# Latent attention: how the reciprocal softmax sums of two items reach the partitions of the output, by transposes or by way of DRAM

## The chip, the cores and the metric

One core of one Trainium2 chip runs the whole kernel. The metric is the device time of one execution in microseconds (us). Before the change it is 2557.08 us, the median of 3 runs (2555.43 to 2558.92).

## The reference, cut to what matters

The layer is a half-step SwiGLU, two token mixers side by side (2-D neighbourhood attention and latent attention, MLA), their gated merge, and another half-step SwiGLU, in float32. The change lies in the latent attention alone:

```python
def _attend(q, k, v):
    s = jnp.einsum('bqhd,bkhd->bhqk', q * q.shape[-1] ** -0.5, k).astype(jnp.float32)
    p = jax.nn.softmax(s, axis=-1).astype(v.dtype)
    return jnp.einsum('bhqk,bkhd->bqhd', p, v)
...
    o_mla = _blocked_attention(q_mla, k_mla, v_mla)
```

There are 8 heads, 1024 latent queries, 1280 keys (256 of context and 1024 latent), 96 channels in a query and a key, and 64 in a value.

## The kernel before, in words

Both attentions run in one loop over 64 **items** (`todo`): items 0 to 31 are neighbourhood attention (8 heads of 4), items 32 to 63 are latent attention (8 heads of 4 blocks of 256 queries). An item has three stages, and the loop overlaps them. In pass n of the loop, the values stage of item n is issued in five parts; between the parts the scores stage of item n+3 (`AHEAD = 3`) is issued, also in five steps; and the softmax steps of item n+2, which its scores stage left in the list `soft` one pass earlier, are handed out over the parts. So a latent item m has its scores in pass m-3, its exponentials in pass m-2 and its values in pass m.

*Scores* (`MlaItem.scores`): the first step multiplies the 256 queries with the context keys, into one bank of PSUM, and needs the tiles of `qh`, `ql` and `kvc`. The next four steps multiply with the latent keys, two halves for each 128 queries, and need `kh` and `kl` too. Each product is three matmuls, since every operand is held as a high and a low part. VectorE copies each bank to SBUF and takes row maxima on the way (`copy_max`, line 1966).

*Softmax*: four exponentials on ScalarE (line 2105) sum their rows as they go; `total` adds the sums and takes the reciprocal on VectorE (lines 2108 and 2109). Two items, 2k and 2k+1, share one 128 x 4 tile of reciprocals, `sums`: queries on partitions, and four columns for two items of two times 128 queries. The sum is not applied to the probabilities but to the output, at the end.

*Values* (`MlaItem.values`): each part transposes four 128 x 128 blocks of probabilities on TensorE (line 164), ScalarE copies them to SBUF as the high part (line 2131), VectorE makes the low part (line 2132), and two parts later (`LAG = 2`) TensorE multiplies them with the values (line 161, tile `bv`). After the fifth part, `head_out` finishes the item: the output stands with value channels on 64 partitions and queries along the row, so the reciprocals, which stand with queries on partitions, have to be turned into a row of 256 and repeated on 64 partitions.

Before, this goes in three steps for a pair of items. GpSimd widens the 128 x 4 tile to 128 x 256 (`widen`, line 1954; it is put in an unused tile named `rope`). In `head_out` of the even item, TensorE transposes it in two pieces into the free half of the output's PSUM bank (lines 1931 and 1932), and two copies bring the two items' rows to SBUF (lines 1934 and 1935). Then, for both items, a copy and an addition join the output's two halves (lines 1938 and 1939), and GpSimd multiplies with the row and splits the result (lines 1940 to 1943). Copies are on ScalarE, in the last four items on VectorE.

*Loads.* All DMAs are issued by SyncE (SP), one after the other in the order in which they are written down; a DMA that has to wait holds back those behind it. `MlaHead` issues fourteen of them for a head: twelve for queries and keys (`qh`, `ql`, `kvc`, `kh`, `kl`), the last two of which are `kl`, and two for values. It is called in pass n where n is a multiple of 4, for the next head, whose first scores are in pass n+1. The query and key tiles (pool `w`, and `kc` or `x`) have room for two heads, so SyncE can issue a head's loads as soon as the head before the last has done its last scores, a whole head ahead of their use. Tile names in the profile are those of the pools: `w`, `kc`, `x`, `l`, `p`, `z` are tiles of a head, `bs`, `bm`, `bv` banks of PSUM, `xu` and `t` working tiles, `st` small columns, `d` scratch in DRAM.

A scheduler places the instructions of each engine from this program; TensorE's and SyncE's keep the written order in this stage, while VectorE's and ScalarE's may be moved a few places.

Of the kernel before, what the change touches and what calls it, by code (L numbers as in the profile page):

```python
# [8 lines left out]
F32 = mybir.dt.float32  # L9
# [6 lines left out]
P = 128  # L16
# [6 lines left out]
NH = 8  # L23
# [15 lines left out]
def f32(ap):  # L39
    return ap.bitcast(F32)  # L40
# [3 lines left out]
def hybrid_block(ctx: ExitStack, tc: tile.TileContext, a: dict, out: bass.AP):  # L44
# [9 lines left out]
    pools = {}  # L54

    def nm(s):
        count[0] += 1
        return f"{s}_{count[0]}"

    def open_pool(key, name, bufs, side):  # L60
        pools[key] = tc.alloc_tile_pool(name=nm(name), bufs=bufs, side=side, reuse_waits="tile")

    def close_pools(*keys):
        for key in keys:
            pools.pop(key).release()

    def U(dt=F32, key="u"):
        return pools[key].tile([P, 1024], dt, tag="u", name=nm("x" + key))
# [7 lines left out]
    def T2(dt=F32, n=512):  # L76
        return pools["t"].tile([P, n], dt, tag="t", name=nm("t"))

    def ST(n=1):
        return sp.tile([P, n], F32, tag=f"st{n}", name=nm("st"))  # L80

    def DR(shape):
        n = nm("d")
        return dp.tile(shape, F32, tag=n, name=n)
# [3 lines left out]
    def PB(tag):  # L88
        return ps.tile([P, 512], F32, tag=tag, name=nm("b" + tag), bufs=PBUFS[tag])
# [17 lines left out]
    def pin(i):  # L107
        if pinned[0]:
            tc.keep_in_program_order(i)
        return i  # L110
# [20 lines left out]
    def put(dst, src):  # L131
        return pin(nc.sync.dma_start(dst, src))
# [30 lines left out]
    def turn_(o, x, i):  # L163
        return pin(nc.tensor.transpose(o, x, i))  # L164

    def mm3(o, s, m, start, stop):
        mmul(o, s[0], m[0], start=start, stop=False)
        mmul(o, s[0], m[1], start=False, stop=False)
        mmul(o, s[1], m[0], start=False, stop=stop)
# [1076 lines left out]
    o = len(plan.main)  # L1246
# [64 lines left out]
    o = len(plan.main)  # L1311
# [12 lines left out]
    o, tail = down1.plan(plan)  # L1324
# [111 lines left out]
    def emit_lat(d, ci, x, bank):  # L1436
        t, sq = T2() if bank else x, T2()

        def high():
            if bank:  # L1440
                act.copy(t, x)
            store(cqT[d][:, ci * 512:(ci + 1) * 512], t)
            act.activation(sq, t, AF.Square)
            later(add, 1)

        def add():
            if ci in squares:
                vec.tensor_tensor(squares[ci], squares[ci], sq, op=ALU.add)
            else:
                squares[ci] = sq  # L1450
        later(high)

    for p in range(3):
        punits.append(Unit(h2, [wc_cols(2 * p), wc_cols(2 * p + 1)],
                           lambda i, ci, x, bank, p=p: emit_lat(2 * p + i, ci, x, bank)))
# [21 lines left out]
    o = len(plan.main)  # L1477
# [137 lines left out]
    o = len(plan.main)  # L1615
# [139 lines left out]
    def na_loads(h):  # L1755
        heads["na", h] = x = NaHead()
        yield from x.loads(h)
# [97 lines left out]
    o = va_at  # L1855
# [9 lines left out]
    o = len(plan.main)  # L1865
# [4 lines left out]
    o = len(plan.main)  # L1870
# [3 lines left out]
    o = len(plan.main)  # L1874
# [3 lines left out]
    o = len(plan.main)  # L1878
# [6 lines left out]
    def na_next(h, n=1):  # L1885
        if h not in na_open:
            na_open[h] = na_loads(h)
        for _ in range(n):
            next(na_open[h], None)
# [31 lines left out]
    def head_out(pv, n, h, hi, lo, shape):  # L1921

        b, c = (0, 64) if h % 2 == 0 else (64, 0)
        copy = nc.vector.tensor_copy if n >= len(todo) - 4 else nc.scalar.copy
        t = T2()
        o, rb = t[b:b + 64, :256], t[b:b + 64, 256:512]
        if n % 2 == 0:  # L1930
            for i in range(2):
                turn_(pv[:, 256 + i * P:256 + (i + 1) * P], wide(n)[:, i * P:(i + 1) * P], ident)
            other = held[0] = T2()
            copy(rb, pv[0:64, 256:512])
            copy(other[b:b + 64, :256], pv[64:128, 256:512])
        else:
            rb = held[0][b:b + 64, :256]
        copy(o, pv[c:c + 64, :256])  # L1938
        nc.vector.tensor_tensor(o, o, pv[b:b + 64, :256], op=ALU.add)
        nc.gpsimd.tensor_tensor(o, o, rb, op=ALU.mult)  # L1940
        o = shape(o)
        nc.gpsimd.tensor_copy(hi[b:b + 64], o)
        nc.gpsimd.tensor_tensor(lo[b:b + 64], o, f32(hi[b:b + 64]), op=ALU.subtract)

    sums, held = {}, [None]

    def wide(n):

        return rope.rearrange("p a b -> p (a b)")[:, (n // 2) % 2 * 256:(n // 2) % 2 * 256 + 256]

    def widen(n):

        x = sums[n // 2].rearrange("p (x i o) -> p i x o", i=2, o=1).to_broadcast([P, 2, 2, 64])
        nc.gpsimd.tensor_copy(wide(n).rearrange("p (i x c) -> p i x c", i=2, x=2), x)

    def sums_of(n):
        if n // 2 not in sums:
            sums[n // 2] = ST(4)
        return sums[n // 2][:, (n % 2) * 2:(n % 2) * 2 + 2]
# [5 lines left out]
    def copy_max(dst, src, m):  # L1965
        nc.vector.tensor_scalar(dst, src, 1.0, FMIN, op0=ALU.mult, op1=ALU.max, accum_out=m)  # L1966
# [5 lines left out]
    class NaItem:  # L1972
# [3 lines left out]
        def scores(self):  # L1976
# [30 lines left out]
            if self.n % 2:  # L2007
                soft.append(lambda: widen(self.n))
            yield

        def values(self):
# [36 lines left out]
            def edge():  # L2048
                turned(((0, 0), (1, 2)), eh, el)

                def w():
                    weigh(pv[0], vt(0), [x[:, 0:256] for x in (eh, el)], False, False)
                    weigh(pv[0], vt(3), [x[:, 128:384] for x in (eh, el)], False, True)
                    hi, lo = [o.rearrange("p (s r j c) -> p s r j c", s=2, r=8, j=4)[:, :, :, j, :] for o in ona[h // 2]]
                    head_out(pv[0], self.n, h, hi, lo, lambda t: t.rearrange("p (s r c) -> p s r c", s=2, r=8))
                return w
# [22 lines left out]
    class MlaItem:  # L2079
# [3 lines left out]
        def scores(self):  # L2083
            hd, b = self.head, self.b
            cx = PB("s")
            m, n_, l, r = ST(8), ST(2), ST(4), sums_of(self.n)
            self.prl, self.prc = prl, prc = [U(), U()], T2()
            qq = [[x[:QK, b * 256 + s * P:b * 256 + (s + 1) * P] for x in (hd.qh, hd.ql)] for s in range(2)]
            for s in range(2):
                mm3(cx[:, s * 256:(s + 1) * 256], qq[s], [hd.kvc[:QK, 0:256], hd.kvc[:QK, 256:512]], True, True)  # L2090
            for s in range(2):
                copy_max(prc[:, s * 256:(s + 1) * 256], cx[:, s * 256:(s + 1) * 256], m[:, 3 * s + 2:3 * s + 3])
            yield
            for s in range(2):
                for e in range(2):
                    lat = PB("s")
                    mm3(lat, qq[s], [x[:QK, e * 512:(e + 1) * 512] for x in (hd.kh, hd.kl)], True, True)
                    copy_max(prl[s][:, e * 512:(e + 1) * 512], lat, m[:, 3 * s + e:3 * s + e + 1])
                    if s + e < 2:
                        yield  # L2100
            nc.vector.tensor_reduce(n_, m[:, 0:6].rearrange("p (s c) -> p s c", s=2), axis=AX.X, op=ALU.max, negate=True)

            def exp(x, i):
                s = i % 2
                nc.scalar.activation(x, x, AF.Exp, bias=n_[:, s:s + 1], accum_out=l[:, i:i + 1])  # L2105

            def total():
                nc.vector.tensor_tensor(r, l[:, 0:2], l[:, 2:4], op=ALU.add)
                nc.vector.reciprocal(r, r)

            for s in range(2):
                soft.append(lambda s=s: exp(prl[s], s))
                soft.append(lambda s=s: exp(prc[:, s * 256:(s + 1) * 256], 2 + s))
            soft.append(total)
            if self.n % 2:
                soft.append(lambda: widen(self.n))
            yield

        def values(self):
# [28 lines left out]
    soft, started = [], []  # L2148
# [25 lines left out]
    close_pools("u", "t")  # L2174
    open_pool("o", "heads", 16, "right")
    open_pool("p", "values", 2, "right")
    na_next(0)
    open_pool("t", "half", 12, "right")
    open_pool("u", "units", 10, "right")
# [81 lines left out]
        fm.step()  # L2261
    pinned[0] = False

    close_pools("u", "t", "p", "z", "x", "y", "l", "kc", "w")
    open_pool("t", "half", TBUFS, "left")
    open_pool("u", "units", 24, "left")

# [41 lines left out]
    for d in range(KD):  # L2309
        o = len(plan.main)  # L2310
# [52 lines left out]
    o = len(plan.main)  # L2363
# [13 lines left out]
    o = len(plan.main)  # L2377
# [14 lines left out]
    o, tail = down2.plan(plan)  # L2392
# [134 lines left out]
```

## Time and profile before

| what | value |
| --- | --- |
| median of 3 runs | 2557.08 us (2555.43 to 2558.92) |
| profiled execution, first to last instruction (its span) | 2553.0 us; it has no other time of its own |
| granted TensorE clock, mean | 0.999 |
| TensorE matmul, busy | 2524.7 us (99%) |
| TensorE weight load, busy | 2146.5 us (84%) |
| VectorE, busy | 1904.4 us (75%) |
| ScalarE, busy | 1238.4 us (49%) |
| GpSimd, busy | 239.4 us (9%) |
| chain of waits, share of TensorE | 87% |

Times in the profile are counted from the start of the span. The latent items fill about 1454 to 1740 us of it. "PE" is a matmul of TensorE, "PEld" its weight load, DVE VectorE, ACT ScalarE, POOL GpSimd, SPq SyncE's queue of DMAs. The median of the runs lies 4.1 us above the profiled execution's span.

### The profile page before, as it was taken

How to read it: one execution, taken by the hardware profiler on the slowest of the kernel's cores; microseconds unless marked ns; L12 is line 12 of the kernel's file. 1: busy time of each engine (PE TensorE's matmuls, PEld its weight loads, DVE VectorE, ACT ScalarE, POOL GpSimd, SP SyncE). 2: the span in 40 equal slices, each digit the busy share in tenths (PEclk: the TensorE clock that was granted, in tenths of full speed). 3: DMA queues.
4: the chain of work that ended last, by engine and by line, in shares of the span. 5: the costliest groups of instructions: out<-in, count | busy, mean ns of one | idle time of the engine just before them, and what ended most of it. 6: DMA issues, size and time to landing. Idle time of an engine off the chain costs nothing.

```text
span 2553.0 us, 38188 instructions
## 1 busy us (share of the span) xinstructions
PE 2524.7 (99%) x13007; PEld 2146.5 (84%) x13007; DVE 1904.4 (75%) x3652; ACT 1238.4 (49%) x2384; POOL 239.4 (9%) x421
## 2 busy tenths in 40 slices
PE   8999999999999999999999999999999999999998
PEld 6888888888888888889889999988888888888887
DVE  5788887898567687874568988886445888777557
ACT  6622223555346643433438888772355322233633
POOL 1000000000002200001006622220030000000000
PEclk9999999999999999999999999999999999999999
DMA  8477765779576665666899823205135667557655
GB/s 314 161 244 234 243 224 188 274 247 294 182 241 221 245 224 188 226 229 203 277 284 249 233 67 77 77 28 214 67 131 179 212 223 236 183 185 259 240 202 194
DMA packets 275477, 523.33 MB, mean 205 GB/s; under 512 B 33425, under 2 KB 84433, under 8 KB 275281
## 3 DMA queue, kind: packets, MB, share of 16 engines
q1 hardware_dynamic: 275280, 520.88, 61.3%
q8 instruction: 103, 1.69, 0.3%
q14 instruction: 94, 0.76, 0.1%
HBM read 375.47 MB, written 145.29 MB: 204 GB/s over the span
## 4 chain that ended last, share of the span: by engine, by line
PE 87%; ACT 5%; DVE 4%; issue 2%; DMA 1%; SPq 0%; POOL 0%; DVEq 0%; POOLq 0%; ACTq 0%
PE bs L161 33%; PE bm L161 30%; PE bv L161 20%; PE bm L164 2%; ACT xu L2105 2%; PE bs L164 1%; DVE xu L1966 1%; DVE t L2132 1%; ACT t L2131 1%; ACT xu L2004 1%; DVE xv L120 1%; DMA xv<-in_wada 0%; ACT t L2105 0%; ACT t L1938 0%; PE bv L164 0%
## 5 line engine op out<-in xcount | busy, mean ns | idle before, releaser
L120 ACT CAST xu<-t 128x512 fp32r<-128x512 f32 x589 | 345.6, 618 | 669.8 <-DVE t L120 556.1
L161 PE MATMUL bm<-xu,xu 128*128 128x512 f32 (+1 forms) x2442 | 596.5, 389 | 0.5 <-ACT t L120 0.4
L161 PEld LDWEIGHTS bm<-xu,xu 128*128 128x128 f32 x2442 | 450.4, 188 | 91.6 <-ACT t L120 1.7
L120 DVE TENSOR_TENSOR xu<-t,xu 128x512 fp32r<-128x512 f32 x589 | 382.8, 686 | 78.3 <-ACT xu L120 78.0
L161 PE MATMUL bs<-xu,xu 128*128 128x512 f32 (+2 forms) x1581 | 388.4, 385 | 0.0
L161 PE MATMUL bs<-xv,xu 128*128 128x512 f32 x1512 | 363.6, 390 | 0.2 <-DVE t L120 0.2
L161 PEld LDWEIGHTS bs<-xu,xu 128*128 128x128 f32 x1581 | 291.9, 188 | 57.8
L161 PE MATMUL bv<-xv,xu 128*128 128x512 f32 x1342 | 336.1, 390 | 0.0
L161 PEld LDWEIGHTS bs<-xv,xu 128*128 128x128 f32 x1512 | 283.6, 188 | 59.5 <-issue 1.0
L161 PEld LDWEIGHTS bv<-xv,xu 128*128 128x128 f32 x1342 | 251.7, 188 | 51.9
L120 DVE TENSOR_TENSOR xu<-xu,xu 128x512 fp32r<-128x512 f32 x282 | 189.5, 687 | 59.9 <-ACT xu L120 58.9
L120 DVE TENSOR_TENSOR t<-t,t 128x512 f32<-128x512 f32 (+4 forms) x350 | 221.0, 634 | 13.9 <-ACT t L120 8.7
L161 PE MATMUL bv<-xu,xu 128*128 128x512 f32 x722 | 191.5, 390 | 0.0
L120 ACT CAST xu<-xu 128x512 fp32r<-128x512 f32 x282 | 169.2, 619 | 15.2 <-DMA xu<-in_f1w 8.9
L120 POOL TENSOR_SCALAR st<-st 128x1 f32<-128x1 f32 x56 | 23.8, 425 | 1581.9 <-ACT t L120 1234.4
L161 PEld LDWEIGHTS bv<-xu,xu 128*128 128x128 f32 x722 | 135.6, 188 | 28.0
L161 PE MATMUL bm<-t,xu 128*128 128x256 f32 (+1 forms) x920 | 156.9, 333 | 0.0
L161 PEld LDWEIGHTS bm<-t,xu 128*128 128x128 f32 x920 | 137.7, 189 | 18.3
L161 PE MATMUL bs<-w,w 96*128 96x512 f32 (+1 forms) x384 | 145.0, 406 | 3.9 <-DVE st L1995 2.1
L2132 DVE TENSOR_TENSOR t<-bm,t 128x512 fp32r<-128x512 f32 x160 | 109.6, 687 | 28.5 <-ACT t L2131 28.1
L164 PE MATMUL bm<-ident,xu 128*128 128x128 f32 x826 | 126.5, 272 | 0.0
L1966 DVE TENSOR_SCALAR_CACHE_REDUCE xu<-bs 128x512 f32<-128x512 f32 (+1 forms) x186 | 110.2, 599 | 2.3 <-PE bs L161 2.1
(256 smaller groups left out, 3376.3 us busy)
## 6 DMA issues: line engine op xcount, KB each, us to landing
d<-t SPq DMA_DIRECT2D x432, 256.0 KB, 2.9
t<-d SPq DMA_DIRECT2D x348, 256.0 KB, 4.9
xu<-in_f1w SPq DMA_DIRECT2D x104, 512.0 KB, 4.4
xu<-in_f2w SPq DMA_DIRECT2D x58, 512.0 KB, 4.6
t<-in_wada SPq DMA_DIRECT2D x112, 256.0 KB, 4.9
t<-in_f1w SPq DMA_DIRECT2D x77, 256.0 KB, 4.8
t<-in_f2w SPq DMA_DIRECT2D x77, 256.0 KB, 5.2
xu<-in_winT SPq DMA_DIRECT2D x36, 512.0 KB, 5.4
```

The source lines that it names most:

```text
L120: return lambda *x, **y: pin(f(*x, **y))
L161: return pin(nc.tensor.matmul(o, s, m, start=start, stop=stop, skip_group_check=open_group[0]))
L164: return pin(nc.tensor.transpose(o, x, i))
L1966: nc.vector.tensor_scalar(dst, src, 1.0, FMIN, op0=ALU.mult, op1=ALU.max, accum_out=m)
L2004: soft.append(lambda s=s: nc.scalar.activation(pr[s][:, :640], pr[s][:, :640], AF.Exp, bias=n_[:, s:s + 1], accum_out=l[:, s:s + 1]))
L2105: nc.scalar.activation(x, x, AF.Exp, bias=n_[:, s:s + 1], accum_out=l[:, i:i + 1])
L2131: nc.scalar.copy(t[0], pb)
L2132: nc.vector.tensor_tensor(t[1], pb, f32(t[0]), op=ALU.subtract)
```

## The change

For the latent items, `widen` and the two transposes with their two copies go. In their place, when the odd item's reciprocals are there, `spread_sums` writes the 128 x 4 tile to DRAM, turned (128 partitions of 4 single floats become 4 rows of 128), and reads the 512 floats back as one row that is repeated on 64 partitions, into a new tile `r`. GpSimd's multiplication takes its factor from `r`. The neighbourhood items keep the old way. The new pool of two 128 x 512 tiles is opened between `values` and `half`.

```diff
@@ head_out
         o, rb = t[b:b + 64, :256], t[b:b + 64, 256:512]
-        if n % 2 == 0:
+        if n >= 4 * NH:
+            rb = spread_rows[n // 2][b:b + 64, (n % 2) * 256:(n % 2) * 256 + 256]
+        elif n % 2 == 0:
             for i in range(2):
                 turn_(pv[:, 256 + i * P:256 + (i + 1) * P], wide(n)[:, i * P:(i + 1) * P], ident)
@@ after widen
+    spread_rows = {}
+    lrow = [DR([4, P]) for _ in range(2)]
+
+    def spread_sums(n):
+
+        b, d = (n // 4) % 2 * 64, lrow[(n // 2) % 2]
+        put(d.rearrange("c p -> p c"), sums[n // 2])
+        t = spread_rows[n // 2] = pools["r"].tile([P, 512], F32, tag="r", name=nm("r"))
+        put(t[b:b + 64, :], d.rearrange("(o c) p -> o (c p)", o=1).to_broadcast([64, 512]))
@@ MlaItem.scores
             soft.append(total)
             if self.n % 2:
-                soft.append(lambda: widen(self.n))
+                soft.append(lambda: spread_sums(self.n))
@@ pools
     open_pool("p", "values", 2, "right")
+    pools["r"] = tc.alloc_tile_pool(name=nm("rows"), bufs=2, side="right", reuse_waits="tile")
```

Counted over the program, TensorE loses 32 transposes, ScalarE 28 copies, VectorE 4 copies and GpSimd 16, and SyncE gains 32 DMAs.

This is SyncE's queue before, where the loads of the third latent head (items 40 to 43) follow those of the second: `z` takes the second head's values, and `w` and `l` the third head's queries and keys, of which seven stand here.

```order
L132 DMA z_15455<-d_348 128x8x128
L132 DMA z_15454<-d_348 128x2x128
L132 DMA w_15940<-d_338 64x1024
L132 DMA w_15940<-d_341 32x1024
L132 DMA l_15944<-d_344 64x256
L132 DMA l_15944<-d_347 32x256
L132 DMA w_15941<-d_338 64x1024
```

And this is the same place now, with `st` the reciprocals, of items 34 and 35 first and of items 36 and 37 after them.

```order
L132 DMA z_15462<-d_348 128x8x128
L132 DMA z_15461<-d_348 128x2x128
L132 DMA d_350<-st_15310 128x4x1
L132 DMA r_15628<-d_350 64x512
L132 DMA d_349<-st_15537 128x4x1
L132 DMA r_15860<-d_349 64x512
L132 DMA w_15941<-d_338 64x1024
L132 DMA w_15941<-d_341 32x1024
L132 DMA l_15945<-d_344 64x256
```

Two pairs of DMAs, each with a write that takes what VectorE made and a read that takes what the write left, now stand in front of a head's loads; before the second latent head there is one such pair.

On ScalarE the scheduler moved some steps as well. Before, in the pass whose softmax is that of item 39 (`xu` and `t` with `st` are its four exponentials, `t` from `bm` the copies of transposed probabilities, `t` from `bv` the copies of `head_out`):

```order
L2105 ACTIVATE xu_15885,st_15884<-xu_15885,st_15883 128x1024
L2105 ACTIVATE t_15887,st_15884<-t_15887,st_15883 128x256
L2131 CAST t_16041<-bm_16036 128x512
L2105 ACTIVATE xu_15886,st_15884<-xu_15886,st_15883 128x1024
L1934 COPY t_16055<-bv_15960 64x256
L1935 COPY t_16058<-bv_15960 64x256
L1938 COPY t_16055<-bv_15960 64x256
L2131 CAST t_16071<-bm_16066 128x512
L2105 ACTIVATE t_15887,st_15884<-t_15887,st_15883 128x256
```

Now, in the same pass (lines are 12 higher in the changed kernel at these places, 2 at line 1938):

```order
L2117 ACTIVATE xu_15886,st_15885<-xu_15886,st_15884 128x1024
L2117 ACTIVATE t_15888,st_15885<-t_15888,st_15884 128x256
L2117 ACTIVATE xu_15887,st_15885<-xu_15887,st_15884 128x1024
L2117 ACTIVATE t_15888,st_15885<-t_15888,st_15884 128x256
L2143 CAST t_16042<-bm_16037 128x512
L1940 COPY t_16056<-bv_15961 64x256
L2143 CAST t_16067<-bm_16062 128x512
```

Two copies are gone, and the last two exponentials stand ahead of a copy of transposed probabilities. On VectorE the sum and the reciprocal of the same item moved up with them, ahead of the `copy_max` of the next head's first scores. This is so in seven passes, for items 35, 39 and on to 59.

More of the change, by code (lines that the diff above doesn't have):

```diff
@@ L2262, in hybrid_block @@
     pinned[0] = False
-    close_pools("u", "t", "p", "z", "x", "y", "l", "kc", "w")
+    close_pools("u", "t", "r", "p", "z", "x", "y", "l", "kc", "w")
     open_pool("t", "half", TBUFS, "left")
```

## The prediction

> **What bounds the kernel now.** I read the page first, then busy time by stretches, one for each latent head.
>
> ```profile
> PE 2524.7 (99%) x13007; PEld 2146.5 (84%) x13007; DVE 1904.4 (75%) x3652; ACT 1238.4 (49%) x2384; POOL 239.4 (9%) x421
> 1480.37:1513.05 32.68, 32.68 (x239) 30.70 (x238) 28.02 (x81) 26.70 (x60) 8.20 (x14) 1.00 0.29 75
> 1513.05:1546.27 33.22, 33.02 (x239) 30.69 (x238) 27.85 (x85) 26.83 (x60) 8.04 (x14) 1.00 0.28 74
> ```
>
> The columns of a stretch are its length, then busy time of PE, PEld, DVE, ACT and POOL, the clock, the DMA share and GB/s. TensorE works through nearly all of a head, and the DMA engines are three tenths busy. So a microsecond off TensorE here is worth a microsecond, and a microsecond for which TensorE waits costs one. The timeline of TensorE shows the beat:
>
> ```profile
> 1513.05 0.96 PE L161 MATMUL bs<-l,w 96*128 96x256 f32 x6
> 1515.01 0.39 PE L161 MATMUL bs<-kc,w 96*128 96x512 f32 x1
> 1515.94 0.38 PE L164 MATMUL bv<-ident,rope 128*128 128x128 f32 x2
> 1516.16 0.60 PE L164 MATMUL bm<-ident,xu 128*128 128x128 f32 x4
> 1521.39 0.96 PE L161 MATMUL bs<-l,w 96*128 96x256 f32 x6
> 1529.45 0.96 PE L161 MATMUL bs<-l,w 96*128 96x256 f32 x6
> ```
>
> "bs<-l,w x6" is the first score step of an item. From 1521.39 to 1529.45 an item takes 8.06 us; from 1513.05 to 1521.39, with the two transposes of `rope` in it, 8.34.
>
> **What is removed.** The two transposes start at 1515.94 and the next at 1516.16: a pair costs 0.22 us of TensorE, though each is listed at 271 ns, since they overlap. 16 pairs make 3.5 us, all of it on the path. The other steps removed:
>
> ```profile
> L1954 POOL COPY rope<-st 128x256 f32<-128x256 f32 x15 | 5.9, 397 | 3.6 <-DVE st L2109 3.5
> L1935 ACT COPY t<-bv 64x256 f32<-64x256 f32 x14 | 5.2, 368 | 0.2
> L1934 ACT COPY t<-bv 64x256 f32<-64x256 f32 x14 | 5.0, 357 | 0.1
> PEld bv L161 <- DVE t L2132: 6.0, 15, 1.2
> ```
>
> The last row is from the waits of 1476 to 1737 us. The copies take some 0.73 us of ScalarE in each pair and GpSimd's widening 0.4; neither engine is the bound, so by themselves these are worth nothing. But what ScalarE finishes sooner lets line 2132 finish sooner, for which TensorE's weight loads wait 6.0 us in all. An item pair without stalls takes 2 x 8.06 + 0.22 = 16.34, a head 32.68, which is just the first head stretch above; the second is 0.54 longer. So at most about 0.5 us a head, 4 us in all, can go with the copies. I take 3, which makes the gain 6.5 us; its bounds are 3.5 and 7.5.
>
> **What is added on SyncE.** The reciprocals' write waits for VectorE, its read waits for the write, and the next head's loads stand behind both. SyncE does hold its queue for such waits:
>
> ```profile
> SPq L132 <- PE bv L161: 140.6, 9, 22.6
> ```
>
> Before, the wait that held a head's loads was for the head before the last, and they came with plenty of time. Here are the first and the last pair of the fourth head's loads, and how long the last pair, `kl` in tile `x`, took to land:
>
> ```profile
> 1512.19 1.08 SPq L132 DMA_DIRECT2D w<-d  x2
> 1517.84 1.08 SPq L132 DMA_DIRECT2D x<-d  x2
> L132 SPq DMA_DIRECT2D x<-d x2: 450/516/582, 1517.8 to 1518.3; - x2
> DMA to landing us min/median/max: 4.0/4.0/4.1
> ```
>
> From the first issue to the landing of the twelfth load is 1518.3 + 4.0 - 1512.2 = 10.1 us. These tiles are first used at 1546.27, 34 us after that first issue; nobody waits.
>
> Now the first issue comes after the reciprocals that are made in the pass before the loads' place in the program (those of items 33, 37, 41 and on to 57). Rows of these, and the matmul that is the first to take the next head's `kl`:
>
> ```profile
> 1473.74 0.15 DVE L2109 RECIPROCAL st<-st 128x2 f32<-128x2 f32 x1
> 1482.33 0.39 PE L161 MATMUL bs<-kc,w 96*128 96x512 f32 x1
> 1504.90 0.15 DVE L2109 RECIPROCAL st<-st 128x2 f32<-128x2 f32 x1
> 1538.51 0.16 DVE L2109 RECIPROCAL st<-st 128x2 f32<-128x2 f32 x1
> 1548.22 0.39 PE L161 MATMUL bs<-x,w 96*128 96x512 f32 x1
> 1672.08 0.16 DVE L2109 RECIPROCAL st<-st 128x2 f32<-128x2 f32 x1
> 1681.82 0.39 PE L161 MATMUL bs<-kc,w 96*128 96x512 f32 x1
> ```
>
> The room is 8.6 us for the second head, 10.1 for the third (1504.90 to 1515.01, quoted above), 9.7 for the fourth and for the eighth, and I take 9.7 for the three between. Into that room must go: the reciprocal, 0.2; the write until it has landed; the issue of the read, 0.5 (the pace of the loads, 516 ns); and the twelve loads, 10.1. The write does not exist before; the nearest rows are these:
>
> ```profile
> d<-t SPq DMA_DIRECT2D x26, 128.0 KB, 2.7
> d<-xu SPq DMA_DIRECT2D x12, 512.0 KB, 5.1
> L132 SPq DMA_DIRECT2D z<-d x2: 583/1303/2023, 1453.4 to 1455.5; - x2
> DMA to landing us min/median/max: 2.0/2.9/3.7
> ```
>
> The shortest of these, a small load, is 2.0 us; the slowest kind of store is 5.1; I take 2.7, the smallest store from 128 partitions, since ours is small in bytes but in 512 pieces of 4. No gain below 2.0 is plausible, as no DMA of these rows is faster.
>
> The Trainium skill speaks against this write: "DMA: Bandwidth & Descriptors", section "Rules for kernel authors", says that a last dimension that isn't contiguous becomes one descriptor for every element. The same page, section "Anatomy of one DMA", gives about 2.0 us of fixed cost for a DMA of GpSimd's path; an estimate with that would put the write at the low end. No row here shows 4-byte stores.
>
> So the loads are complete 0.2 + 2.7 + 0.5 + 10.1 = 13.5 us after the reciprocal, and TensorE, which has only this order, stands for 13.5 - 9.7 = 3.8 us at five heads, 3.4 at the third and 4.9 at the second: 27.3 us in all. It stands in two steps, first for `kvc` in the first score step and then for `kh` and `kl`. With 2.0 for the write it is 22.4, with 5.1 it is 44.1.
>
> **Other edits.** The read of `r` lands well before its use: the pair's reciprocals at 1504.90 and the old transposes at 1515.94 are 11 us apart, and write and read need some 6 to 7. The other pair of DMAs of a head (items 35, 39 ...) waits in front of nothing that is due. A head's value loads come later but are used three passes on. The tail's loads of `wo` stand behind the last pairs and have some 20 us of room. I cost these at nothing.
>
> The moved exponentials, seven times, are on VectorE's path:
>
> ```profile
> 1514.71 1.15 ACT L2105 ACTIVATE xu<-xu,st 128x1024 f32<-128x1024 f32 x1 [0.73 <-DVE st L2101]
> 1515.86 0.49 ACT L2105 ACTIVATE t<-t,st 128x256 f32<-128x256 f32 x1
> 1515.19 0.42 DVE L1966 TENSOR_SCALAR_CACHE_REDUCE t<-bs 128x256 f32<-128x256 f32 x1
> ```
>
> The sum now stands where VectorE was at 1515.19, and the second pair of exponentials ends about 1514.71 + 2 x 1.64 = 1518.0: VectorE stands 2.8 us, and `copy_max`, the low parts and the PSUM banks behind it wait. It is the very pass in which TensorE stands for the loads, so I cost it at nothing. Without that cover it costs between 0 and 2.8 us a time; I would take 1, since VectorE has 5.4 us idle in a head, so 7 us.
>
> **The sum.** 27.3 - 6.5 = 20.8 us: a span of 2573.8 and, with the 4.1 us between span and median, 2577.9, rounded to 2578. With the bounds it runs from 22.4 - 7.5 = 14.9 (2572) to 44.1 - 3.5 = 40.6 (2598).
>
> **The rivals.**
> - *The loads hide after all, and it gets faster.* SyncE's wait matters only once the twelfth load lands over 9.7 us after the reciprocal. If the reciprocal came 4 us sooner against TensorE's beat, the gain would stand alone: 2557.1 - 6.5 = 2550.6. Against it: the twelve loads alone take 10.1 us. 7%.
> - *The stalls help themselves.* While TensorE stands, ScalarE and VectorE catch up, and with two copies fewer the next reciprocal comes sooner, by up to 2 us I judge. Then each stall is 2 us shorter: 27.3 - 14 - 6.5 = 6.8, 2564. For it: ScalarE's copies stand ahead of the last exponential. Against it: the first head stretch above has no stalls, and the reciprocal in it, at 1504.90, has a room of 10.1 us instead of 9.7, a gain of only 0.4. 12%, half of it within 0.2% of before.
> - *The clock falls.* If a stall made TensorE run at half speed for as long as two parts of an item (8.06 / 5 x 2 = 3.2 us), seven stalls add 22 us: 2600. A stall of 2.56 us is in the trace, and the clock of its stretch stayed at 1.00:
>
> ```profile
> 1347.98 0.50 PE L161 MATMUL bs<-kc,w 128*128 128x256 f32 x2 [2.56 <-DVE st L1995]
> 1320.00:1460.00 140.00, 133.10 (x1002) 127.44 (x1001) 122.47 (x414) 116.33 (x278) 87.43 (x169) 1.00 0.89 241
> ```
>
>   Ours come in two steps of some 2 us with work between. 8%. The Trainium skill, "TensorE: Matmul & The Clock Gate", Part 1, has the clock halved after an idle window of about 3.4 us; by that rule, too, two short steps keep it.
>
> **How the numbers follow.** The forecast has 73%, the rivals the 27% above. A measurement of this kernel tells about 0.2%, 5 us, from no change. Faster by more than that: 0.07; within: 0.06; slower: 0.87. The range, 2565 to 2602, holds the forecast's bounds and the clock's case, and reaches nearly to the case in which the stalls help themselves.
>
> **What would show it.** In the profile after, TensorE should wait for DMAs into `w`, `l`, `p`, `z`, `kc` or `x` at the start of seven heads, some 27 us in all; SyncE should wait for VectorE's reciprocals; a head's stretch should be about 36 us long, not 33; the write should land in about 2.7 us. It is wrong if TensorE never waits for a DMA there, or if its waits are for VectorE.

## The result and the profile after

The changed kernel takes 2637.56 us (median of six executions), 81.8 us more than the 2555.81 us of the kernel before on the same chip: a ratio of 1.0318, with a 95% interval of 1.0306 to 1.033. One of the six executions, at 3713.74 us with a granted clock of 0.642, was a slow one and is left out of the ratio. The forecast was 2578. The direction was right; the size was not, and the range (2565 to 2602) missed it.

Two lines of the profile's page after the change: busy time by engine, and the granted clock of TensorE in 40 slices, of which the latent heads are slices 23 to 28.

```profile
PE 2542.0 (97%) x12975; PEld 2160.3 (82%) x12975; DVE 1911.1 (73%) x3648; ACT 1234.2 (47%) x2356; POOL 233.5 (9%) x405
PEclk9999999999999999999999888989999999999999
```

TensorE has 32 matmuls fewer, as it should (two transposes for each of 16 pairs), and yet is busy 17 us longer; its clock falls where the latent heads are. Next, busy time by stretches. The first row is the stretch that I use for all comparisons, from the first score step of item 35 to that of item 63, 28 items; the other is a single head.

```profile
1473.51:1787.26 313.75, 248.18 (x1628) 228.51 (x1625) 205.98 (x589) 183.37 (x397) 53.88 (x87) 0.87 0.29 63
1490.92:1535.78 44.86, 35.88 (x233) 33.25 (x233) 29.14 (x84) 25.97 (x56) 7.43 (x12) 0.84 0.29 60
```

The same 28 items in the kernel before:

```profile
1472.28:1705.00 232.72, 231.68 (x1655) 214.80 (x1654) 197.97 (x590) 187.47 (x423) 59.03 (x101) 1.00 0.26 68
```

This stretch alone is 81.0 us longer, so all of the loss is here. Length less TensorE's busy time is the time in which TensorE stands, that is, does nothing: 65.6 us after, 1.0 before. The waits in the latent heads (columns: total, times, longest), TensorE's first and then SyncE's, say for what:

```profile
PE bs L161 <- DMA z<-d: 28.8, 6, 9.1
PE bs L161 <- DMA l<-d: 18.2, 4, 7.7
PE bs L161 <- DMA p<-d: 18.1, 4, 8.0
...
SPq L132 <- DMA d<-st: 144.6, 16, 10.9
SPq L132 <- DVE st L2121: 109.5, 8, 18.4
```

TensorE waits for the next head's queries and context keys, and SyncE spends 9.0 us for each of 16 pairs on the landing of the write. SyncE's queue in front of the third head shows it in order of time:

```profile
1520.04 0.36 SPq L132 DMA_DIRECT2D d<-st  x1
1528.77 0.45 SPq L132 DMA_DIRECT2D r<-d  x1
1529.31 1.17 SPq L132 DMA_DIRECT2D w<-d  x2
```

The write is issued at 1520.04 and the read 8.73 us later. What do the DMA engines do in the meantime? The DMA view of 1520.5 to 1528.0 in 40 slices of 0.19 us (the first line is the busy share in tenths), and below it the write's time to landing:

```profile
DMA  0057000000000000000000000000000000000000
DMA packets 528, 0.00 MB, mean 0 GB/s; under 512 B 528, under 2 KB 528, under 8 KB 528
...
d<-st SPq DMA_DIRECT2D x1, 2.0 KB, 8.7
```

All packets (512 pieces of 4 bytes, and 16 more) run in two slices, by about 1521.3. The other 7.4 us are no transfer: the write has been sent and isn't yet confirmed. TensorE meanwhile:

```profile
1535.78 0.55 PE L161 MATMUL bs<-l,w 96*128 96x256 f32 x1 [7.49 <-DMA l<-d]
1537.81 1.40 PE L161 MATMUL bs<-l,w 96*128 96x256 f32 x5 [1.48 <-DMA l<-d]
1539.87 1.06 PE L164 MATMUL bm<-ident,xu 128*128 128x128 f32 x4
1530.20:1543.70 13.50, 6.44 (x26) 5.95 (x26) 2.65 (x11) 3.82 (x10) 0.00 (x0) 0.50 0.84 190
```

It stands 7.49 and then 1.48 us. Behind that, four transposes take 1.06 us where they took 0.60 before, since the clock of this stretch (last row, last number but two) is 0.50.

### The profile page after: what moved, and what is told of

It is laid out like the page before. It is cut to its first block, busy times and chain, and to the rows that moved or that the text cites. A ratio compares the mean times of both kernels' runs of the same rounds, so it can differ in the third digit from the quotient of the medians.

```text
span 2632.5 us, 38154 instructions
## 1 busy us (share of the span) xinstructions
PE 2542.0 (97%) x12975; PEld 2160.3 (82%) x12975; DVE 1911.1 (73%) x3648; ACT 1234.2 (47%) x2356; POOL 233.5 (9%) x405
## 4 chain that ended last, share of the span: by engine, by line
PE 87%; DMA 5%; ACT 3%; DVE 3%; issue 1%; SPq 0%; POOL 0%; DVEq 0%; POOLq 0%; ACTq 0%
PE bs L161 34%; PE bm L161 29%; PE bv L161 20%; PE bm L164 2%; DMA d<-st 2%; PE bs L164 1%; ACT xu L2016 1%; DMA r<-d 1%; DVE xv L120 1%; SPq L132 0%; DVE xu L1978 0%; DMA z<-d 0%; ACT t L2038 0%; ACT t L120 0%; DMA l<-d 0%
## 5 line engine op out<-in xcount | busy, mean ns | idle before, releaser
L2143 ACT CAST t<-bm 128x512 fp32r<-128x512 f32 x160 | 92.5, 582 | 120.3 <-PE bm L164 117.6
```

The source lines that it names most:

```text
L2143: nc.scalar.copy(t[0], pb)
```

## The experiments

All with their median, the ratio to the kernel before, and for the stretch of 28 items its length, the time that TensorE stands and the clock, from the view by stretches.

| kernel | us | ratio (95%) | length | stands | clock |
|---|---|---|---|---|---|
| before | 2555.8 | | 232.7 | 1.0 | 1.00 |
| after | 2637.6 | 1.0318 (1.0306 to 1.033) | 313.8 | 65.6 | 0.87 |
| rows16 | 2579.9 | 1.0095 (1.008 to 1.011) | 262.5 | 19.4 | 0.94 |
| gpq | 2610.7 | 1.0214 (1.0197 to 1.0231) | 284.5 | 31.1 | 0.93 |
| read_late | 2615.9 | 1.0235 (1.022 to 1.025) | 296.7 | 50.1 | 0.90 |
| warm | 2634.3 | 1.031 (1.0294 to 1.0325) | 315.4 | 24.5 | 0.94 |
| rows16_split | 2572.0 | 1.0067 (1.0053 to 1.0081) | 251.2 | 14.4 | 0.97 |
| rows16_gpq | 2556.7 | 1.0003 (0.9994 to 1.0011) | 234.4 | 2.6 | 1.00 |
| no_pair | 2553.2 | 0.9993 (0.9984 to 1.0001) | 231.2 | 0.2 | 1.00 |
| no_pair_dvecopy | 2547.8 | 0.9965 (0.9952 to 0.9977) | 225.7 | 0.0 | 1.00 |
| rows16_gpq_dve | 2550.7 | 0.9981 (0.9972 to 0.999) | 229.3 | 0.5 | 1.00 |

The theory after the result: the place on SyncE's queue costs what the forecast said, but the write takes 8 to 10 us and not 2.7. The rivals: the place costs by itself, or other edits do.

**Larger pieces (rows16).**

```diff
-    lrow = [DR([4, P]) for _ in range(2)]
-        put(d.rearrange("c p -> p c"), sums[n // 2])
-        put(t[b:b + 64, :], d.rearrange("(o c) p -> o (c p)", o=1).to_broadcast([64, 512]))
+    lrow = [DR([P, 4]) for _ in range(2)]
+        put(d, sums[n // 2])
+        put(t[b:b + 64, :], d.rearrange("(o p) c -> o (p c)", o=1).to_broadcast([64, 512]))
```

> The changed kernel with one thing different: the scratch in DRAM is 128 rows of 4, so the write is 128 pieces of 16 bytes and not 512 pieces of 4 in 4 rows, and the row that comes back is read through a strided view. Everything keeps its place on SyncE. Theory A (the write's time was mis-sized, the place on the queue was judged rightly): the write lands in about 2.5 us and not 8 to 10, TensorE stands 3 to 5 us a head in two short steps, its clock stays full, and the time is what the forecast gave for a write of that length, 2570 to 2585 us. Rival B (the place on the queue costs by itself, whatever the write takes): the write lands sooner, but TensorE still stands over 7 us in one piece at the start of a head, with half the clock behind it, and the time stays above 2610 us.

Measured: 2579.9 us, as theory A has it (the profiled execution, 2583.7, is the slowest of four). In the stretch, and SyncE's waits for the write:

```profile
1474.10:1736.57 262.47, 243.09 (x1627) 223.92 (x1626) 205.36 (x589) 182.74 (x397) 57.72 (x87) 0.94 0.32 75
...
SPq L132 <- DMA d<-st: 29.0, 16, 3.3
```

SyncE now waits 1.8 us for a write instead of 9.0, and TensorE stands 19.4 us. That the clock stays full was wrong. Here are TensorE's rows at the start of the second head, and the clock of the 6.5 us behind them:

```profile
1483.48 0.35 PE L161 MATMUL bs<-z,w 96*128 96x256 f32 x1 [1.04 <-DVE st L2117]
1485.50 1.41 PE L161 MATMUL bs<-z,w 96*128 96x256 f32 x5 [1.66 <-DMA z<-d]
1485.00:1491.50 6.50, 6.00 (x25) 5.55 (x25) 2.51 (x10) 2.66 (x7) 0.00 (x0) 0.50 0.81 179
```

Two short stands, 1.04 and 1.66 us with 0.35 us of work between, were enough for half speed.

**Another queue (gpq).** Both DMAs go to `nc.gpsimd.dma_start`, with the 4-byte write as it was.

```diff
-        put(d.rearrange("c p -> p c"), sums[n // 2])
+        nc.gpsimd.dma_start(d.rearrange("c p -> p c"), sums[n // 2])
```

> The changed kernel, with both transfers of the reciprocals issued from GpSimd's queue and not SyncE's. The write keeps its 512 pieces of 4 bytes. Theory A (all of the loss is that the next head's loads stand behind the two transfers): TensorE waits for no DMA in the latent heads, the clock stays full, and only the gain is left, 6.5 to 8 us: 2548 to 2551 us. Rival B (part of the loss is in other edits, the moved exponentials or GpSimd's multiplication waiting for a late row): the loads come in time, but TensorE waits for VectorE or for the units of the first pair, and the time is 2555 us or more.

Measured: 2610.7 us, so theory A fell. TensorE waits for no DMA, but for the casts of the value step; GpSimd's row shows why, and the DMA view of 1516 to 1532 (slices of 0.4 us) shows something else:

```profile
PE bv L161 <- ACT t L2143: 19.8, 11, 3.5
PE bv L161 <- DVE t L2144: 12.5, 27, 3.5
...
1516.18 0.80 POOL L1964 DMA_DIRECT2D d<-st  x1 [1.00 <-DVE st L2121]
1526.55 0.55 POOL L1966 DMA_DIRECT2D r<-d  x1 [9.57 <-DMA d<-st]
1527.11 0.74 POOL L1942 TENSOR_TENSOR t<-t,r 64x256 f32<-64x256 f32 x1
...
GB/s 0 0 0 78 195 168 317 345 313 188 40 0 0 0 0 0 0 0 0 0 0 0 72 20 0 123 51 41 41 31 215 346 272 256 264 205 228 202 266 256
w<-d SPq DMA_DIRECT2D x3, 128.0 KB, 7.6
p<-d SPq DMA_DIRECT2D x1, 512.0 KB, 9.6
d<-st POOLq DMA_DIRECT2D x1, 2.0 KB, 10.1
```

GpSimd stands 9.57 us for the landing, in front of its own multiplications, and the chain of waits runs through them. Besides, no data is moved from 1520.4 to 1524.8. For the first part of that time nothing is outstanding, but SyncE issues loads from 1522.04 on, and their first data moves 2.8 us later; in the kernel before it moved 1.2 to 1.4 us after the issue. The 128 KB loads land after 7.6 us (3.3 in the kernel before, and 3.3 in rows16_gpq below, where the same queues are used and the write has 16-byte pieces). A 512 KB load of values, issued at 1516.29, 0.1 us behind the write, and moved by 1520.4, lands only 0.4 us before the write, after 9.6 us. So here the write held transfers of another queue too. The Trainium skill says in "DMA: Bandwidth & Descriptors", section "Queues, rings and completion order", that a transfer's completion is a strongly ordered write, which lands only after every earlier write of the same DMA engine, across its queues; that load agrees with it, at 9.6 against 10.1 us.

**Loads first (read_late).** The read, now a function that is kept in a list, goes behind the next head's loads, and these are written down two parts sooner (the text below says two passes; it is two of the five parts of one pass).

```diff
-        put(t[b:b + 64, :], d.rearrange("(o c) p -> o (c p)", o=1).to_broadcast([64, 512]))
+        reads.append(read)
...
+            if n % 4 == 0 and x == 0 and 8 <= n // 4 and n // 4 + 1 < 2 * NH:
+                ahead_head(n // 4 + 1)
+            if x == 0:
+                while reads:
+                    reads.pop(0)()
```

> The changed kernel with the write at its place on SyncE in front of the next head's loads, but the read put behind these loads, and the latent heads' loads written down two passes sooner in the program, right behind the write. So the loads wait for the reciprocal, not for the landing of the write. Theory A (what holds the loads is the read's wait for the write, 8 to 10 us): the loads land about 9 us sooner, in 0.2 + 0.5 + 10.1 = 10.8 us after the reciprocal against a room of 9.7: TensorE stands 0 to 1.5 us a head, and the time is 2548 to 2562 us. Rival B (the wait for the reciprocal is enough, or the late row now holds GpSimd's multiplication and the units behind it): TensorE still waits 3 us or more a head, and the time is 2575 us or more.

Measured: 2615.9 us, in rival B's range, and TensorE still stands 50.1 us, all but 0.7 of it for the loads; but neither of B's reasons is it. SyncE's queue at the third head, and from the DMA view of 1515 to 1531 the landing of those 128 KB loads of which it is known:

```profile
1515.12 0.36 SPq L132 DMA_DIRECT2D d<-st  x1
1515.58 1.09 SPq L132 DMA_DIRECT2D w<-d  x2
...
1518.96 6.14 SPq L132 DMA_DIRECT2D l<-d  x2
...
w<-d SPq DMA_DIRECT2D x3, 128.0 KB, 11.9
```

And such loads in the kernel before:

```profile
w<-d SPq DMA_DIRECT2D x3, 128.0 KB, 3.3
```

The first loads are issued at once, right behind the write, but one lands only after 11.9 us, and the eighth is out at 1525.1 (1518.96 + 6.14), 10 us after the write. By the trace's operands it waits for the semaphore on which the write counts, and counts on the same one (eight are used in turn on this queue), which would explain that hold; that wasn't tried by itself. Either way the slow write holds the loads, although nobody in front of them waits for its data.

**Busy instead of idle (warm).** 60 transposes of the identity ahead of a head's first score step.

```diff
+            if b == 0 and hd.h:
+                for i in range(60):
+                    turn_(cx[:, (i % 4) * P:(i % 4 + 1) * P], ident, ident)
```

> The changed kernel with 60 needless transposes of the identity in front of the first score step of each of the last seven latent heads; their results are overwritten. They fill most of the time in which TensorE stands for the loads, and move no load. Theory A (about 24 us of the loss is the clock, which is halved after the long stand): the clock stays full in these heads, the stands are as long with the transposes in them, and the time falls by about 20 to 25 us, to 2613 to 2618 us. Rival B (the half clock runs mostly while TensorE would stand or is covered by slack, so the loss is the stands alone): the time stays within 5 us of the changed kernel, 2637 us, or rises.

Measured: 2634.3 us, and the test is inconclusive. The clock of the stretch rose only from 0.87 to 0.94: behind the needless work TensorE still stood in short pieces, up to 2.8 us, and these probably brought the half clock back, as in rows16.

**What makes the write slow (probe).** Eight layouts, one write of each.

```diff
+            if k == 0:
+                put(probe[0].rearrange("c p -> p c"), s)
+            elif k == 1:
+                put(probe[1][:, :, 0:1].rearrange("c p o -> p c o"), s3)
...
+            elif k == 4:
+                put(probe[4].rearrange("(p o) -> p o", o=1), s[:, 0:1])
```

> The 16-byte version on SyncE with one more write of the same sums behind the read of each second pair, each in another layout, read by nobody: 512 pieces of 4 bytes side by side in 4 rows; 512 of 4 bytes each 64 bytes apart; 512 of 4 bytes each 512 bytes apart; 256 of 8 bytes side by side; 128 of 4 bytes side by side; 128 of 4 bytes 64 bytes apart; 256 of 4 bytes side by side; 128 of 16 bytes. What is asked is the time to landing. Theory A (DRAM confirms pieces under a line's size one after the other, since several of them share a line): side by side 512 take 8 to 10 us, 256 about half, 128 a quarter, while 64 or 512 bytes apart they take 2 to 3 us. Theory B (the number of pieces alone counts): 512 take 8 to 10 us at any distance. Theory C (the 4 bytes alone count): 128 pieces of 4 bytes are as slow as 512, and 8 and 16 bytes are fast.

The issues in the order of that list (the last number is the time to landing):

```profile
d<-st SPq DMA_DIRECT2D x1, 2.0 KB, 10.2
d<-st SPq DMA_DIRECT2D x1, 2.0 KB, 2.7
d<-st SPq DMA_DIRECT2D x1, 2.0 KB, 2.8
d<-st SPq DMA_DIRECT2D x1, 2.0 KB, 3.9
d<-st SPq DMA_DIRECT2D x1, 0.5 KB, 7.2
d<-st SPq DMA_DIRECT2D x1, 0.5 KB, 2.4
d<-st SPq DMA_DIRECT2D x1, 1.0 KB, 9.1
d<-st SPq DMA_DIRECT2D x1, 2.0 KB, 2.9
```

512 pieces of 4 bytes take 10.2 us side by side and 2.7 us when they are 64 bytes apart; so neither the number of pieces nor their size is it, but that small pieces lie side by side. B and C fall. Of A the proportions are wrong: 256 side by side still take 9.1 us, not half, and 128 take 7.2, not a quarter. 8-byte pieces side by side take 3.9 and 16-byte pieces 2.9. Each is a single write; what DRAM does with them isn't visible.

**Write on SyncE, read on GpSimd (rows16_split).**

```diff
-        put(t[b:b + 64, :], d.rearrange("(o p) c -> o (p c)", o=1).to_broadcast([64, 512]))
+        nc.gpsimd.dma_start(t[b:b + 64, :], d.rearrange("(o p) c -> o (p c)", o=1).to_broadcast([64, 512]))
```

> The write in 128 pieces of 16 bytes on SyncE at its place, the read on GpSimd's queue. SyncE's loads then wait for the reciprocal and for 0.4 us of the write's issue, and not for its landing. Theory A: the loads are complete 0.2 + 0.4 + 10.1 = 10.7 us after the reciprocal against a room of 9.7: TensorE stands 0.5 to 2 us a head, some 7 us in all, which is about the gain: 2553 to 2562 us. Rival B (any stand in these heads also brings half speed): 2565 us or more. Rival C (GpSimd's wait for the write holds its multiplications): TensorE waits for casts and not for DMAs.

Measured: 2572.0 us, rival B. TensorE stands 14.4 us, twice what A said, and the clock is at 0.97. Why the stands are twice as long stays open.

**Both on GpSimd, 16-byte pieces (rows16_gpq)**, and **neither (no_pair)**, in which `spread_sums` issues nothing:

```diff
-            rb = spread_rows[n // 2][b:b + 64, (n % 2) * 256:(n % 2) * 256 + 256]
+            rb = o
```

> The write in 128 pieces of 16 bytes, and both transfers issued from GpSimd's queue. Theory A (what GpSimd's queue lost with the 4-byte write was its own standing for the landing, 8 to 10 us in front of its multiplications): with a write of about 2.5 us GpSimd stands only so long, TensorE waits neither for DMAs nor for casts, its clock stays full, and the gain of about 7 us is left: 2547 to 2552 us, which would beat both kernels. Rival B (GpSimd's queue costs by itself, since the reciprocal's wait also stands in front of the multiplications): TensorE still waits for the low parts of the value step, and the time is 2558 us or more.

> The changed kernel without the write and the read: the latent items are multiplied by themselves and not by the reciprocals, so their normalization is left out. Everything else, the order of the exponentials too, is the changed kernel's. Theory A (the gain was sized rightly, the moved exponentials cost nothing once nothing stalls): 2547 to 2552 us. Rival B (the moved exponentials need the cover of the load stalls): about 7 us more, 2555 to 2560 us, with VectorE waiting 2.8 us for ScalarE's exponentials once a head and TensorE behind it.

Measured: 2556.7 and 2553.2 us, each between the ranges of its two theories. Neither has a stand worth naming, and neither has the gain: without any transfer the median is only 2.3 us below the kernel before, which is not clear of noise (0.9993, 0.9984 to 1.0001), and the stretch 1.5 us shorter.

One thing that the last text says does not hold: no_pair does not keep the changed kernel's order of the exponentials. Here is ScalarE in the pass of item 39 in no_pair:

```profile
1516.47 0.50 ACT L2113 ACTIVATE t<-t,st 128x256 f32<-128x256 f32 x1
...
1516.96 0.56 ACT L2139 CAST t<-bm 128x512 fp32r<-128x512 f32 x1
1517.43 1.15 ACT L2113 ACTIVATE xu<-xu,st 128x1024 f32<-128x1024 f32 x1
```

A cast of transposed probabilities stands among the exponentials again, as in the kernel before. The same holds for gpq and rows16_gpq: the scheduler moved the exponentials only in the kernels in which SyncE's queue waits for the reciprocals. So no_pair says what transposes and copies are worth by themselves, and nothing of the moved exponentials.

The missing gain isn't lost once a head either: items take 8.06 us only at first (five of them) and then 8.28 and 8.35 by turns, in every head. In no_pair the waits of 1481 to 1705, of the weight loads and then of ScalarE and VectorE:

```profile
PEld bv L161 <- DVE t L2140: 6.2, 22, 0.4
...
ACT xu L2113 <- DVE st L2109: 35.9, 27, 1.5
ACT t L2139 <- POOL xo L1945: 9.4, 20, 0.5
...
DVE t L2140 <- ACT t L2139: 17.1, 55, 0.5
```

TensorE waits for VectorE's low parts, these for ScalarE's casts; they wait for GpSimd at times, and stand in one row with exponentials that wait for VectorE's maxima.

**The ring of half tiles** was one suspect: `open_pool("t", "half", 14, "right")` for 12 (no_pair_t14 and before_t14), an unused `T2()` in every second item (no_pair_rot), and 13 tiles with one row buffer (rows16_gpq_t13).

> The kernel without write and read (normalization of the latent items left out, they are multiplied by themselves), with 14 buffers in place of 12 for the half tiles of the latent stage. Asked is where the gain went: without transposes, copies and transfers the items still took 8.28 to 8.35 us and not 8.06, with ScalarE's casts waiting for GpSimd about 0.5 us an item. Theory A (the cast waits for a half tile that GpSimd's last operations still hold: an item now takes exactly 12 such tiles, so a ring of 12 gives each step the same tile every time): with 14 the waits go and the items take 8.06: 2546 to 2550 us. Rival B (the order of VectorE and ScalarE itself sets 8.3 us): unchanged, 2552 to 2555 us.

> The kernel without write and read (normalization of the latent items left out), with 12 buffers, but with one half tile more taken and not used in every second item, as the kernel before took one for its copies. So an item pair takes 25 of them again, and the ring turns by one each pair. Theory A (the fixed ring is what costs): 2546 to 2550 us. Rival B: unchanged, 2552 to 2555 us.

> The kernel before with 14 buffers for the half tiles and not 12. If the half tiles hold the latent items of the kernel before too, it falls by 2 to 3 us, to about 2553; if its items are set by the transposes and by VectorE's low parts alone, it stays within 1 us of 2555.5.

> The 16-byte version on GpSimd's queue with one row buffer in place of two and 13 half tiles in place of 12 (the space is no more). Theory A (the ring of 12 holds its items, at 8.28 and 8.59 us by turns): the items fall towards 8.06 and the time to 2548 to 2553 us, below both kernels. Rival B (GpSimd's own standing for the write, or the single row buffer, holds them): 2555 us or more.

Measured: 2550.8 us (0.9978, 0.9969 to 0.9987), 2553.2 (0.9987, 0.9978 to 0.9996), 2554.9 (0.9996, 0.9986 to 1.0005) and 2563.6 (1.0029, 1.0017 to 1.004). With 14 tiles the casts' waits for GpSimd are gone, but the items still take 8.23 and 8.34 us and the stretch is only 0.5 us shorter. The median lies further down, 5.5 us below the kernel before and between the ranges of A and B, but not by these items. So the ring isn't what holds the items. Why 13 tiles with one row buffer are slower stays open.

**Which engine holds them (no_pair_noadd, no_pair_dvecopy).** Work off VectorE, or off ScalarE:

```diff
-        nc.vector.tensor_tensor(o, o, pv[b:b + 64, :256], op=ALU.add)
+        if n < 4 * NH:
+            nc.vector.tensor_tensor(o, o, pv[b:b + 64, :256], op=ALU.add)
```

```diff
-        copy = nc.vector.tensor_copy if n >= len(todo) - 4 else nc.scalar.copy
+        copy = nc.vector.tensor_copy if n >= 4 * NH else nc.scalar.copy
```

> The kernel without write and read (normalization of the latent items left out), also without VectorE's addition of the two halves of the output in these items (0.42 us an item). Its 14 us of the forecast's gain are not asked, only what holds the items at 8.28 us. Theory A (VectorE's row of work is the longest in an item, with ScalarE waiting for it): the items fall to 8.06 and the time to 2545 to 2549 us. Rival B (ScalarE's row is the longest): within 1.5 us of 2553.

> The kernel without write and read (normalization of the latent items left out), with the copy of an item's output half on VectorE and not on ScalarE: 0.36 us less for ScalarE, about 0.4 us more for VectorE in each item. Theory A (VectorE's row is the longest): slower by some 5 to 13 us, 2558 to 2566 us. Rival B (ScalarE's row is the longest, as VectorE's last waits are for its casts): the items fall to 8.06 and the time to 2545 to 2549 us.

(The 14 us in the first text are a slip; the forecast's gain was 6.5.) Measured: 2558.9 us (1.0012, 1.0003 to 1.0021) and 2547.8. With 0.36 us of copy off ScalarE every item takes 8.06 us:

```profile
1471.93:1697.64 225.71, 225.71 (x1627) 211.78 (x1626) 212.01 (x619) 169.44 (x370) 50.61 (x87) 1.00 0.26 70
```

TensorE is busy from end to end, and 225.7 us is what 28 items cost when nothing waits. So the copy in ScalarE's row of work held them: rival B of the second text. The first test has neither of its outcomes: less work for VectorE made the items longer (8.54 us), which isn't explained; ScalarE then waited 42.2 us for VectorE's maxima in place of 35.9. So it isn't the amount of an engine's work alone.

**The whole (rows16_gpq_dve, before_dve).** The copy moved, with the pair as in rows16_gpq, and in the kernel before.

> A complete kernel: write in 128 pieces of 16 bytes, both transfers on GpSimd's queue, and the copy of a latent item's output half on VectorE and not on ScalarE. Theory A (the stalls were the write's landing on SyncE, and what then held the items at 8.3 to 8.6 us was ScalarE's copy, ahead of its casts): the items take 8.06 us, TensorE never waits, 2546 to 2550 us, below both kernels. Rival B (GpSimd's standing for the write still holds the items): 2553 us or more.

> The kernel before with one edit, the copy of a latent item's output half on VectorE and not on ScalarE. Theory A (in the kernel before too ScalarE's copies hold TensorE, by the 3 us above the transposes): 2551 to 2553 us, as 3.5 us of transposes stay. Rival B (the copies of the transposed sums, which stay on ScalarE, hold it in every second item): within 1 us of 2555.5.

Measured: 2550.7 us, 4.7 below the kernel before on its chip, and 2555.3 (0.9999, 0.9991 to 1.0008). So a gain of 4.7 us belongs to the row by way of DRAM together with the moved copy; neither has it alone. In before_dve most items take 8.06 us or, with the transposes, 8.28, but the first item of a head (40, 44 and on to 60) now takes 9.1 to 9.3 (no item of the kernel before takes over 8.8), so nothing is gained. In rows16_gpq_dve, whose time is just above A's range, 15 of the 28 items still take 8.14 us or more:

```profile
1473.22:1702.49 229.27, 228.80 (x1628) 211.50 (x1626) 214.50 (x616) 167.78 (x370) 72.01 (x114) 1.00 0.30 77
```

## Why the prediction was wrong

- **The write, 2.7 us (bounds 2.0 to 5.1): the step that failed.** It took 8.7 us in the place quoted, and the upper bound, taken from a large store, was no bound for a store in 4-byte pieces side by side. The rest of that step holds: with 8.7 the forecast's sum is 0.2 + 8.7 + 0.5 + 10.1 - 9.7 = 9.8 us at five heads, 9.4 at the third and 10.9 at the second, 69.3 us; TensorE stood 65.6. In rows16 the writes in front of the seven heads' loads landed in 1.4 to 2.4 us, 11.5 in all where the forecast has 18.9; the sum then gives 27.3 - 7.4 = 19.9 us, and TensorE stood 19.4. The mechanism, the place on the queue, was right; the price was that of another kind of store. That rows16 also met the forecast's time is partly chance: its stands were shorter than forecast, and its clock cost what was left out (next point). The Trainium skill's sentence on one descriptor for every element ("DMA: Bandwidth & Descriptors", section "Rules for kernel authors") was weighed in the forecast: the trace agrees (512 pieces, and 16 packets more), but the probe shows that the count isn't what costs.
- **The clock, left out of the sum at 8%: the second step that failed.** The stands came in one piece of 7.5 us and one of 1.5, and TensorE then ran at half speed. By the rows above, TensorE was busy 248.2 us in the stretch, against 225.7 for the same work when nothing waits: 22.5 us, nearly the 22 of that rival, which the forecast left out of its sum. In rows16 it was 243.1 - 225.7 = 17.4. The forecast argued from one stall of 2.56 us with a clock of 1.00 over 140 us. That reading was right for that execution, but one execution was too little. The same stall is in the changed kernel, where the mean over the same 140 us is 0.99. The 3.2 us behind it read after, and before:

```profile
1349.30:1352.50 3.20, 3.09 (x13) 3.09 (x14) 1.60 (x9) 1.74 (x4) 1.60 (x4) 0.50 0.93 217
```

```profile
1349.30:1352.50 3.20, 3.20 (x30) 3.20 (x29) 2.61 (x11) 2.76 (x8) 1.29 (x3) 1.00 1.05 214
```

  One and the same stall brings half speed in one execution and not in another. From 1347 to 1360 us the clock is 0.87 in the profiles of after, gpq, no_pair, rows16_gpq and no_pair_dvecopy, and 1.00 in those of before and rows16.
- **The gain, 6.5 us: right here, under a condition that the forecast did not see.** Before, TensorE was busy 231.7 us and stood 1.0; without waits it needs 225.7: 7.0 us, all of it gained between the stands, where items take 8.06 us. The forecast took 3 us of its gain for what ScalarE finishes sooner, and did not ask what ScalarE's remaining steps would hold. Without the stands no_pair gains 1.5 us in the stretch. The likely reason is that the stands let ScalarE catch up, since in no_pair too the first five items take 8.06 us; no run shows it by itself.
- **The sum.** 65.6 of stands + 22.5 of clock - 7.0 of gain are 81.1 us, and the stretch is 81.0 longer. That the terms add up is no proof, since a stretch is its busy time and its stands. What they say is where the forecast's 20.8 us went wrong: 38.3 us too little for the stands, 22.5 left out for the clock, and 0.5 the other way for the gain.
- **The moved exponentials, at nothing.** This was right, as far as it was seen: in the changed kernel VectorE waits for the last exponentials, up to 2.8 us a time as forecast (the row is from 1440 to 1830 us), and the wait at the third head, which ends at 1533.10, lies inside TensorE's stand of 7.49 us:

```profile
DVE st L2120 <- ACT t L2117: 20.0, 8, 2.8
```

  What they cost without that cover (7 us in the forecast) stays open, since no kernel here has them moved and no stands.
- **What would show it.** The waits for the tiles named, SyncE's waits for the reciprocals and the longer heads came as said; in place of 27 us of waits, 36 us a head and 2.7 us for the write it was 65, 45 and 8.7.

## What to carry to other kernels

Here a small store was priced by how its pieces lie in DRAM; when the profile has no store of the form that is added, the upper bound has to stay open: measure one, or lay it out in longer pieces. A wait put on a queue costs what stands behind it, and a store that lands late can hold other transfers as well: here it did for loads on its own queue (read_late) and on another (gpq). When the work on the bounding engine is cut, ask which engine's order is next. Read the clock in windows as short as the stall, and in more than one execution. And when an experiment leaves something out, check in its trace that the rest kept its order.

## What the runs showed of the hardware

- Writes to DRAM of 4-byte pieces side by side: 512 land after 8.2 to 10.4 us in the changed kernel, though all are sent within about 0.4; 64 bytes apart, 2.7; in 16-byte pieces on SyncE's queue, 1.4 to 3.8 (rows16 and probe).
- While such a write was unconfirmed, the first data of loads on another queue moved 2.8 us after their issue instead of 1.2 to 1.4, and 128 KB loads landed after 7.6 us instead of 3.3 (gpq); on the same queue one took 11.9 (read_late).
- TensorE's half speed came after stands as short as 1.04 and 1.66 us close together, and lasted 6.5 us at least (rows16). The Trainium skill, "TensorE: Matmul & The Clock Gate", Part 1, speaks of an idle window of about 3.4 us; here less idle time than that, 2.7 us in two pieces, was enough.
